# A two-layer encoder on one core: the opening laid out anew, the softmax's sums applied to the gates as rows, weight splits in pieces of 512 columns with half of the high parts on ScalarE, and a new order of issue

## The chip, the cores and the metric

The kernel runs on one core of a Trainium2 chip. The metric is the device time in microseconds (us) of one execution; lower is better. The core's engines are PE (TensorE), DVE (VectorE), ACT (ScalarE), POOL (GpSimd) and SP (SyncE, which here only issues DMAs). Each engine takes its instructions in the order in which they were issued and waits on semaphores of the others.

## The reference

All is float32; the sequence has 1024 tokens of width 1024, batch 1.

```python
c_act = jax.nn.silu(c)
for layer in range(DEPTH):                       # DEPTH = 2
    mod = c_act @ ada_w[layer] + ada_b[layer]
    shift, scale, gate = jnp.split(mod, 3, axis=-1)
    h = rms_norm(x, norm_w[layer]) * (1.0 + scale[:, None, :]) + shift[:, None, :]
    ...                                          # y = even_mixer(h) or odd_mixer(h)
    x = x + gate[:, None, :] * y
```

The result is the final RMSNorm of x. The even mixer (layer 0) projects h and runs two groups of attention side by side: A, eight query heads of 64 on two key and value heads, with rotary positions by row and column; and B, eight heads of latent attention, with compressed queries and a compressed key and value. Each is a dense softmax over all 1024 keys,

```python
p = jax.nn.softmax(sc, axis=-1)
oa = oa * jax.nn.silu(ga)
ob = mla_attention(q_lat, q_rope, ckv, k_rope, w_uv) * jax.nn.silu(gb)
return jnp.concatenate([oa, ob], axis=-1) @ w_out
```

and the outputs go through gates and one output projection. The odd mixer (layer 1) is attention in a window of 128 tokens to each side, with a penalty by distance and a learned sink per head, 16 heads on 4 key and value heads, then gate and output projection.

## The kernel before

**Products.** The data stay transposed, features on the 128 partitions. Every large product is made of three (`mm3`, L1112): a float32 operand is split into a high part (a cast to fp32r) and a low part (what is left), and high·high, high·low and low·high are added in PSUM. So each operand needs a cast and a subtraction on ACT, POOL or DVE before PE can use it. In the names an `h` or `l` at the end is the high or low part (`w30h`, `G7l`), and an `s` the weight as loaded (`wg7s`).

**Who decides the order.** All operations pass through `Recorder` (L586), which is why every row of the profile has one line, L1017 before: rows are told apart by the tiles. It records the operations, plans them with a cost for each (`cost`, L695), with pools of buffers (`u`: 52 tiles of 128x1024, `ua`: 3 of 128x512, `sm`: 32 of 128x16, eight PSUM banks) and with a rule (`held`, L932) by which a DVE operation with two inputs in SBUF and a POOL operation don't run at once. The order planned is then changed by hand: `placed` (L961) puts operation i right behind operation j for every pair of the table `PLACES` (L81), and `emit` (L1009) issues the result.

**Stages**, by the trace of before:
- 0 to 21 us, the opening. SP loads x by four chunks of two times 512 columns (`xT`), the small columns (`cols`), the first modulation weights (`ada`) and the first projection weights (`w30s`, `w10s`). PE runs transposes of the identity (`warm`, L1151), and turns SiLU(c) into the row `cb`. `xT_half` (L1358) squares x on ACT, adds halves on POOL and DVE (`sq`), and sums over partitions on PE, with a column `share` of 1/1024 as the moving operand (`mean_squares`, L1222): matmuls of 128x1. DVE adds epsilon (`ss`), POOL raises to the power −1/2 (`r`), PE transposes r into rows (`broadcast_rstd`, L1246), DVE multiplies x by them and ACT applies shift and scale (`modulate`, L1290, out: `hT00h`). The shift and scale of a chunk are sums of `ada` times `cb` on DVE, one 128x1024 operation each (`ada_sum`, L1186).
- 21 to 128 us: layer 0's projections; `wload` (L1318) loads and splits their weights.
- 128 to about 350 us: the gates' product by a scheme of seven products for eight. `g_load` (L1701) splits its weights (`wg0` to `wg15`, double tiles of 128x1024), `combine` (L1680) builds its sums of h (`hf`, `G4` to `G7`, `gk`) on DVE, `g_step` (L1741) issues the matmuls between those of attention. The gates stay in `gT`.
- 132 to 640 us: 16 groups A, then 16 groups B (`run_groups`, L1854), each one head and half the queries. `softmax_unit` (L1803) makes one tile of 128 queries by 1024 keys: PE's scores, DVE's maximum (`nm`), ACT's exponential with its sum (`Pa`, `Pb`, `sm`), DVE's reciprocal (`rs`), and POOL scales the tile by it. In the next group `pv_step` (L1832) transposes P by 128 keys, splits it (`hla`, `hlb`) and multiplies by V; for two of eight key tiles in groups B that is done ahead on POOL (`pv_ahead`, L1822). `pv_final` (L1844) adds two halves of the accumulator (`ot`, `og`) and POOL multiplies by the gate, 64 rows at a time.
- 640 to 705 us: layer 0's output (`wino_out`, L2271; `t30l`, `s30l`, `a220l` are its splits). To 760 us: layer 1's projections (`f_load`, L2498, splits `wf0` and on; `f_step`, L2523). To 1047 us: the windows (`win_S`, L2635, `win_PV`, L2668). To the end: layer 1's output (`xr`) and the last norm (`rbz`).

Weights that are sums of blocks pass through DRAM: POOL issues DMAs that add (`ws`, `gs`, `fs`), SP fetches the results.

Of the kernel before, what the change touches and what calls it, by code (L numbers as in the profile page):

```python
# [54 lines left out]
WARM = (18, 8, 6)  # L55
AHEAD = {"a": {}, "b": {4: 0, 7: 3}}
# [19 lines left out]
G_HI = "pool"  # L76
G_LO = "pool"
# [2749 lines left out]
```

## Time and profile before

| what | value |
|---|---|
| median of 3 runs | 1129.39 us (1127.12 to 1130.62) |
| the profiled execution | 1134.05 us, span 1132.2 us |
| mean granted clock of PE | 0.985 |
| busy: PE, DVE, ACT, POOL | 97%, 86%, 66%, 66% of the span |
| chain that ended last | PE 81%, DVE 12% |
| first product of the projections starts at | 20.75 us |
| POOL busy with scaling P (128 operations) | 154.7 us |
| POOL busy from 200 to 320 us | 107.51 of 120 us |

Busy time of PE counts from the issue of a matmul to its modelled end, so rows of neighbours overlap: what a matmul takes from PE is the distance of its start to the next one's. In a row of the timeline stand start, length, engine, line, operation, tiles written and read, shape, the number of instructions put together, and in brackets how long the engine idled before and what ended that. In a row of waits stand the total, the number of times and the longest.

### The profile page before, as it was taken

The numbers are of one execution on the slowest core, as the hardware profiler recorded it, in microseconds if no ns is written. First come the engines' busy times: TensorE is split into PE (matmuls) and PEld (weight loads), VectorE is DVE, ScalarE is ACT, GpSimd is POOL, SyncE is SP. The second block draws the span as 40 slices with busy tenths as digits, with TensorE's granted clock in tenths as the row PEclk, the third lists the DMA queues.
The fourth block names the chain that finished last, engine by engine and source line by source line (L and its number), as shares of the span: only waits on it lengthen the run. The fifth ranks groups of instructions, "written<-read, shape, count | busy, mean of one in ns | idle before, by whom it ended". The sixth has DMA issues, their size and how long they took to land.

```text
span 1132.2 us, 17617 instructions
## 1 busy us (share of the span) xinstructions
PE 1102.4 (97%) x5928; PEld 942.9 (83%) x5928; DVE 978.1 (86%) x1604; ACT 749.5 (66%) x1460; POOL 745.3 (66%) x732
## 2 busy tenths in 40 slices
PE   8999999999999999999999999999999999999996
PEld 7898877888887988888888877888888888888785
DVE  5978998898999988887888999998877787778995
ACT  4663554778777877887798742667776776766722
POOL 1135777988986737877879736757675775976422
PEclk7999999999999999999999999999999999999997
DMA  9869863564751486974785477401111221349303
GB/s 368 326 201 318 273 252 78 144 195 125 203 165 15 89 289 207 212 204 160 210 238 191 114 271 245 152 1 38 41 54 56 78 68 42 113 166 336 103 1 149
DMA packets 60026, 183.72 MB, mean 162 GB/s; under 512 B 7200, under 2 KB 9632, under 8 KB 58912
## 3 DMA queue, kind: packets, MB, share of 16 engines
q1 hardware_dynamic: 54464, 159.00, 40.2%
q0 software_dynamic: 4608, 22.02, 10.7%
q10 hardware_dynamic: 864, 1.57, 0.4%
q8 instruction: 47, 0.77, 0.3%
q14 instruction: 43, 0.35, 0.1%
HBM read 147.31 MB, written 70.91 MB: 193 GB/s over the span
## 4 chain that ended last, share of the span: by engine, by line
PE 81%; DVE 12%; issue 2%; ACT 2%; POOL 1%; DMA 1%; POOLq 0%; SPq 0%; DVEq 0%; ACTq 0%
PE psum L1017 81%; DVE nm L1017 1%; DVE xr L1017 1%; DVE hla L1017 1%; DVE t30l L1017 1%; DMA xT<-in_xt 1%; ACT Pb L1017 1%; DVE o L1017 0%; DVE T6l L1017 0%; DVE hlb L1017 0%; DVE s31l L1017 0%; DVE s30l L1017 0%; DVE psum L1017 0%; POOL sq L1017 0%; DVE t40l L1017 0%
## 5 line engine op out<-in xcount | busy, mean ns | idle before, releaser
L1017 DVE TENSOR_REDUCE nm<-psum 128x1 f32<-128x1024 f32 x128 | 155.6, 1219 | 21.0 <-PE psum L1017 18.8
L1017 POOL TENSOR_SCALAR Pa<-Pa,rs 128x1024 f32<-128x1024 f32 x64 | 77.4, 1233 | 34.9 <-DVE rs L1017 30.4
L1017 POOL TENSOR_SCALAR Pb<-Pb,rs 128x1024 f32<-128x1024 f32 x64 | 77.3, 1217 | 32.7 <-DVE rs L1017 29.7
L1017 POOL TENSOR_SCALAR p<-p,dn 128x384 f32<-128x384 f32 (+1 forms) x128 | 69.4, 560 | 33.2 <-DVE dn L1017 32.9
L1017 ACT ACTIVATE Pa<-psum,nm 128x1024 f32<-128x1024 f32 x64 | 71.6, 1119 | 27.6 <-DVE nm L1017 26.0
L1017 DVE TENSOR_TENSOR hla<-psum,hla 128x512 fp32r<-128x512 f32 x128 | 82.6, 683 | 4.4 <-ACT hla L1017 4.2
L1017 ACT ACTIVATE Pb<-psum,nm 128x1024 f32<-128x1024 f32 x64 | 71.9, 1124 | 20.2 <-DVE nm L1017 18.0
L1017 DVE CUSTOM_DVE_ANT_0 p<-psum,relt,sinkn 128x384 f32<-128x384 f32 (+1 forms) x128 | 70.4, 579 | 15.3 <-PE psum L1017 13.8
L1017 PE MATMUL psum<-hla,VA 128*128 128x512 f32 x256 | 80.5, 407 | 1.3 <-DVE og('0', 2)_631 L1017 1.1
L1017 ACT ACTIVATE p<-p,nm 128x385 f32<-128x385 f32 (+1 forms) x128 | 74.8, 591 | 10.2 <-DVE nm L1017 5.6
L1017 ACT CAST hla<-psum 128x512 fp32r<-128x512 f32 x128 | 70.5, 596 | 16.3 <-PE psum L1017 15.3
L1017 PE MATMUL psum<-k,q 128*128 128x512 f32 x256 | 80.5, 401 | 0.6 <-ACT Pb L1017 0.6
L1017 PE MATMUL psum<-hlb,VB 128*128 128x512 f32 x256 | 78.3, 409 | 0.5 <-DVE hlb L1017 0.5
L1017 PE MATMUL psum<-ident,Pa 128*128 128x128 f32 x512 | 73.4, 274 | 0.0
L1017 ACT CAST hl<-psum 128x512 fp32r<-128x512 f32 x88 | 48.7, 590 | 34.2 <-PE psum L1017 30.2
L1017 DVE TENSOR_TENSOR hlb<-psum,hlb 128x512 fp32r<-128x512 f32 x96 | 63.2, 684 | 8.7 <-ACT hlb L1017 8.2
L1017 PE MATMUL psum<-ident,Pb 128*128 128x128 f32 x512 | 70.3, 273 | 0.1
L1017 DVE TENSOR_TENSOR hl<-psum,hl 128x512 fp32r<-128x512 f32 x88 | 57.9, 686 | 12.9 <-ACT hl L1017 10.9
L1017 PEld LDWEIGHTS psum<-ident,Pa 128*128 128x128 f32 x512 | 61.4, 141 | 8.4 <-issue 0.2
L1017 PEld LDWEIGHTS psum<-ident,Pb 128*128 128x128 f32 x512 | 60.3, 140 | 9.0 <-ACT Pb L1017 0.5
L1017 ACT COPY ot<-psum 64x512 f32<-64x512 f32 x64 | 37.4, 584 | 39.6 <-PE psum L1017 38.5
L1017 ACT ACTIVATE sq<-xr 128x512 f32<-128x512 f32 (+2 forms) x30 | 19.3, 658 | 61.3 <-DVE xr L1017 61.3
(1152 smaller groups left out, 3845.3 us busy)
## 6 DMA issues: line engine op xcount, KB each, us to landing
ada<-in_ada_t SPq DMA_DIRECT2D x32, 512.0 KB, 8.1
fs<-in_w_f POOLq DMA_DIRECT2D x12, 768.0 KB, 9.2
adag<-in_ada_t SPq DMA_DIRECT2D x16, 512.0 KB, 5.3
ws<-in_w_out POOLq DMA_DIRECT2D x16, 512.0 KB, 6.5
S<-ws SPq DMA_DIRECT2D x16, 512.0 KB, 4.5
A<-in_w_out SPq DMA_DIRECT2D x12, 512.0 KB, 4.5
o<-spill SPq DMA_DIRECT2D x12, 512.0 KB, 5.5
fs<-in_w_f SPq DMA_DIRECT2D x6, 768.0 KB, 8.9
```

The costliest lines, as they stand in the source:

```text
L1017: fn(*[real(v) for v in a], **{k: real(v) for k, v in kw.items()})
```

## The change

**The opening.** ACT does all squares first. POOL adds the halves of chunk 0, DVE those of chunks 1 and 2 and then adds both halves of chunk 3 into chunk 2's sum; PE makes the sum over partitions with 12 calls instead of 20. Eight warming transposes stand before the first of them and 14 between the second and the third chunk's; the eight before r's transposes are gone. The shift of chunk 0 is no longer a DVE operation of 128x1024 but eight matmuls of 128x1 on PE, with an operand `ada_0` of the same size, laid out by the host, and a DVE operation of 128x1. A copy of r by DVE (`got`) stands before DVE's further sums and low parts. The first projection weights `w10` and `w30` come and are split in two halves each.

PE from the program's start, before and then after. `share,sq` are the sums over partitions, `cs,ada` the shift, `ident,r` r's transposes.

```order
L1017 MATMUL psum<-ident 128x128 x18
L1017 MATMUL psum<-ident,cs 128x128 x8
L1017 MATMUL psum<-share,sq_126 128x1 x4
L1017 MATMUL psum<-share,sq_127 128x1 x4
L1017 MATMUL psum<-share,sq_128 128x1 x4
L1017 MATMUL psum<-share,sq_129 128x1 x8
L1017 MATMUL psum<-ident 128x128 x8
L1017 MATMUL psum<-ident,r 128x128 x4
L1017 MATMUL psum<-ident 128x128 x6
L1017 MATMUL psum<-w30h_138,hT00h_91 128x512
```
```order
L1195 MATMUL psum<-ident 128x128 x18
L1195 MATMUL psum<-ident,cs 128x128 x8
L1195 MATMUL psum<-ident 128x128 x8
L1195 MATMUL psum<-share,sq_126 128x1 x4
L1195 MATMUL psum<-share,sq_127 128x1 x4
L1195 MATMUL psum<-ident 128x128 x14
L1195 MATMUL psum<-share,sq_128 128x1 x4
L1195 MATMUL psum<-cs,ada_131 128x1 x8
L1195 MATMUL psum<-ident,r 128x128 x4
L1195 MATMUL psum<-ident 128x128 x6
L1195 MATMUL psum<-w10h_136,hT00h_91 128x416
```

Eight sums over partitions have gone from behind the last square, and the eight matmuls of the shift stand between the mean and r's transposes.

**Layer 0's softmax.** P stays as the exponential. The four sums of a group stand in one tile; one reciprocal of 128x4 per group goes by a DMA on SP to DRAM, and once both heads of a pair have theirs, two DMAs on SP of 64x512 bring them back as rows over the partitions. POOL multiplies the gate by these rows (16 operations of 128x512) and then the heads' outputs by the gate, once per pair of heads (16 of 128x512 instead of 32 of 64x512). The rows take buffers of the pool `ua`, now four.

**Weight splits.** For the gates and for layer 1's features the parts are made in pieces of 512 columns; ACT casts the high parts of the first eight double tiles of each, POOL the others and all low parts.

POOL around the gates' weights `wg4` to `wg8`, before and after; `Pa<-Pa,rs` is the scaling of P.

```order
L1017 TENSOR_SCALAR wg4h<-wg4s 128x1024
L1017 TENSOR_SCALAR wg5h<-wg5s 128x1024
L1017 TENSOR_TENSOR wg4l<-wg4s,wg4h 128x1024
L1017 TENSOR_SCALAR Pa_355<-Pa_355,rs 128x1024
L1017 TENSOR_TENSOR wg5l<-wg5s,wg5h 128x1024
L1017 TENSOR_SCALAR wg6h<-wg6s 128x1024
L1017 TENSOR_TENSOR wg6l<-wg6s,wg6h 128x1024
L1017 DMA ws_317<-in_w_out 128x1024
L1017 TENSOR_SCALAR Pa_359<-Pa_359,rs 128x1024
L1017 TENSOR_SCALAR wg7h<-wg7s 128x1024
L1017 TENSOR_TENSOR wg7l<-wg7s,wg7h 128x1024
```
```order
L1195 TENSOR_TENSOR wg4l<-wg4s,wg4h 128x512 x2
L1195 TENSOR_TENSOR wg5l<-wg5s,wg5h 128x512 x2
L1195 TENSOR_TENSOR wg6l<-wg6s,wg6h 128x512 x2
L1195 TENSOR_TENSOR wg7l<-wg7s,wg7h 128x512 x2
L1195 TENSOR_SCALAR wg8h<-wg8s 128x512 x2
```

Scalings, casts and a DMA have gone from between the subtractions, which now follow each other.

**Order and constants.** `WINDOW` (how far ahead the planner looks) goes from 400 to 300, `SM_BUFS` from 32 to 12, `UA_BUFS` from 3 to 4, `RESERVE` of `sm` from 11 to 2; in `win_S` the maxima and the sums share a tile. `PLACES` has 638 lines instead of 460, and a new table `BANKS` gives PSUM banks by hand. The recorder is the same.

DVE at the end, before and after: `gcol` and `ngcol` are evictions of the last products, `rbz` the last norm's scaling of other columns.

```order
L1017 SCALAR_TENSOR_TENSOR xr_1908<-psum,gcol,xr_1908 128x2x256
L1017 SCALAR_TENSOR_TENSOR xr_1905<-psum,ngcol,xr_1905 128x256
L1017 SCALAR_TENSOR_TENSOR xr_1902<-xr_1902,cols,rbz_1979 128x512 x2
L1017 SCALAR_TENSOR_TENSOR xr_1901<-xr_1901,cols,rbz_1979 128x512
L1017 SCALAR_TENSOR_TENSOR xr_1904<-xr_1904,cols,rbz_1979 128x512
L1017 SCALAR_TENSOR_TENSOR xr_1905<-psum,ngcol,xr_1905 128x256 x2
L1017 SCALAR_TENSOR_TENSOR xr_1906<-psum,ngcol,xr_1906 128x256
```
```order
L1195 SCALAR_TENSOR_TENSOR xr_1709<-psum,gcol,xr_1709 128x2x256
L1195 SCALAR_TENSOR_TENSOR xr_1704<-xr_1704,cols,rbz_1780 128x512
L1195 SCALAR_TENSOR_TENSOR xr_1705<-xr_1705,cols,rbz_1780 128x512
L1195 SCALAR_TENSOR_TENSOR xr_1706<-psum,ngcol,xr_1706 128x256
L1195 SCALAR_TENSOR_TENSOR xr_1709<-psum,gcol,xr_1709 128x2x256
L1195 SCALAR_TENSOR_TENSOR xr_1702<-xr_1702,cols,rbz_1780 128x512
L1195 SCALAR_TENSOR_TENSOR xr_1705<-xr_1705,cols,rbz_1780 128x512
L1195 SCALAR_TENSOR_TENSOR xr_1706<-psum,ngcol,xr_1706 128x256
L1195 SCALAR_TENSOR_TENSOR xr_1707<-psum,ngcol,xr_1707 128x256
```

Of four scalings between the first eviction and the next, two stand ahead of the first now, and an eviction (`gcol`) stands between.

The diff, cut to its core:

```diff
-UA_BUFS = 3
-SM_BUFS = 32
+UA_BUFS = 4
+SM_BUFS = 12
...
-WARM = (18, 8, 6)
-AHEAD = {"a": {}, "b": {4: 0, 7: 3}}
+WARM = (18, 8, 14, 6)
+AHEAD = {"a": {}, "b": {4: 0, 7: 3}, "1": {}}
...
-G_HI = "pool"
-G_LO = "pool"
+G_ACT = 8
+F_ACT = 8
...
 PLACES = (
-    (95, 39), (92, 95), (127, 45), (167, 127), (164, 167), (234, 161), (231, 234), (96, 57), (237, 229), (304, 237),
...
@@ ada_mods
+            if turn and j:
+                s = U("ada0")
+                load(s, ada_0)
+                ps = PA("ada0")
+                for i in range(8):
+                    m_ = mm(ps[:, 0:1], lhsT=s[:, i * P:(i + 1) * P], rhs=cs[:, 8 + i:9 + i], start=i == 0, stop=i == 7)
+                    m_.deps.update(o.i for o in turn)
+                    turn = [m_]
+                marks["turn"] = turn
+                nc.vector.scalar_tensor_tensor(out=mods[:, 2 * k + j:2 * k + j + 1], in0=ps[:, 0:1], scalar=scale, in1=first,
+                                               op0=ALU.mult, op1=ALU.add)
+                continue
...
@@ broadcast_rstd
-        around = warm(WARM[1], around) if around else []
+        if around:
+            got_ = SM("got")
+            marks["got"] = nc.vector.tensor_copy(got_[:, 0:nt], r[:, 0:nt])
+        around = around or []
...
@@ wload
+            if late:
+                for o in (0, n // 2):
+                    c = slice(o, o + n // 2)
+                    load(s[:, c], w[:, c])
+                    nc.scalar.copy(h[:, c], s[:, c])
+                    sub(l[:, c], s[:, c], f(h[:, c]))
+                    rec.ops[-1].deps.add(late.i)
+                    res.append((h[:, c], l[:, c]))
+                continue
...
@@ xT_half
+            for k2 in range(3):
+                nc.scalar.activation(sq[k2], xT[0][k2], AF.Square)
+            for e in range(2):
+                nc.scalar.activation(part(3, e), xT[0][3][:, e * 512:(e + 1) * 512], AF.Square)
+            plus(nc.gpsimd, part(0, 0), part(0, 1))
+            plus(nc.vector, part(1, 0), part(1, 1)).deps.update(o.i for o in copied)
+            plus(nc.vector, part(2, 0), part(2, 1))
...
+            for e in range(2):
+                plus(nc.vector, part(2, 0), part(3, e))
+            m_ = add(part(2, 0), True)
...
+    def parts_of(s, h, l, n, eng):
+
+        for o in range(0, n, 512):
+            c = slice(o, o + 512)
+            if eng is nc.scalar:
+                nc.scalar.copy(h[:, c], s[:, c])
+            else:
+                hi_pool(h[:, c], s[:, c])
+            nc.gpsimd.tensor_tensor(out=l[:, c], in0=s[:, c], in1=f(h[:, c]), op=ALU.subtract)
...
+        parts_of(s, h, l, 1024, nc.scalar if d < G_ACT else nc.gpsimd)
...
@@ softmax_unit
-            nc.scalar.activation(pt, S, AF.Exp, bias=nm[:, 0:1], accum_out=sm[:, 0:1])
+            nc.scalar.activation(pt, S, AF.Exp, bias=nm[:, 0:1], accum_out=sums)
+        return pt
...
-        nc.vector.reciprocal(r[:, 0:1], sm[:, 0:1])
-        nc.gpsimd.tensor_scalar(pt, pt, r[:, 0:1], 1.0, op0=ALU.mult, op1=ALU.mult)
-        return pt
...
+    def keep_sums(p, e, half, sums):
+
+        r = SM("rs")
+        nc.vector.reciprocal(r[:, 0:4], sums)
+        nc.sync.dma_start(out=rs_sp[p][e:e + 1, half * 512:(half + 1) * 512].rearrange("o (q j) -> (o q) j", j=4),
+                          in_=r[:, 0:4])
+        if e:
+            c = slice(half * 512, half * 512 + 512)
+            rows[p, half] = UA(f"rows{p}{half}")
+            for e in range(2):
+                load(rows[p, half][e * 64:e * 64 + 64, :], rs_sp[p][e:e + 1, c].partition_broadcast(64)[:, 0])
+
+    def scale_gate(p, half, gate):
+
+        c = slice(half * 512, half * 512 + 512)
+        by_tile = gate[:, c].rearrange("p (j q) -> p j q", j=4)
+        nc.gpsimd.tensor_tensor(out=by_tile, in0=by_tile, in1=rows.pop((p, half)).rearrange("p (q j) -> p j q", j=4), op=ALU.mult)
...
@@ pv_final
-        nc.gpsimd.tensor_tensor(out=og[r, c], in0=og[r, c], in1=gate[r, c], op=ALU.mult)
+        if h % 2:
+            nc.gpsimd.tensor_tensor(out=og[:, c], in0=og[:, c], in1=gate[:, c], op=ALU.mult)
...
@@ run_groups
+                keep_sums(g["p"], g["h"] % 2, g["half"], sums[:, 0:4])
             if prev is not None:
+                if prev["h"] % 2:
+                    scale_gate(prev["p"], prev["half"], prev["gate"]())
...
@@ f_load
-        hi_pool(h[:, 0:w], s[:, 0:w])
-        nc.gpsimd.tensor_tensor(out=l[:, 0:w], in0=s[:, 0:w], in1=f(h[:, 0:w]), op=ALU.subtract)
+        parts_of(s, h, l, w, nc.scalar if d < F_ACT else nc.gpsimd)
```

More of the change, by code (lines that the diff above doesn't have):

```diff
@@ L1166, in encoder_kernel @@
     cb = U("cb")
-    copied = []
+    copied, turned = [], []
     for j in range(2):
@@ L1315, in modulate, with wload @@
                 nc.scalar.activation(keep, src, AF.Identity, bias=sh_col(l, kc))
-    def wload(ws, ncol, name, hi_eng="pool", mark=None, lo_eng="dve"):
+    def wload(ws, ncol, name, hi_eng="pool", mark=None, lo_eng="dve", late=None):
         res = []
@@ L1363, in xT_half @@
             pt, add = mean_squares("x0", 4)
-            for k2 in range(4):
-                q = U(f"sq0{k2}")
-                a, b = q[:, 0:512], q[:, 512:1024]
-                if k2 < 3:
-                    nc.scalar.activation(q, xT[0][k2], AF.Square)
-                    (nc.vector if k2 == 1 else nc.gpsimd).tensor_tensor(out=a, in0=a, in1=b, op=ALU.add)
-                    if k2 == 1:
-                        rec.ops[-1].deps.update(o.i for o in copied)
-                else:
-                    nc.scalar.activation(a, xT[0][k2][:, 0:512], AF.Square)
-                    nc.scalar.activation(b, xT[0][k2][:, 512:1024], AF.Square)
-                for t in (a,) if k2 < 3 else (a, b):
-                    m_ = add(t, k2 == 3 and t is b)
+            sq = [U(f"sq0{k2}") for k2 in range(4)]
+            part = lambda k2, e: sq[k2][:, e * 512:(e + 1) * 512]
+            plus = lambda eng, a, b: eng.tensor_tensor(out=a, in0=a, in1=b, op=ALU.add)
+            for k2 in range(3):
[5 more added lines that the diff above has]
+            plus(nc.vector, part(2, 0), part(2, 1))
+            w_ = warm(WARM[1], turned)
+            for k2 in range(2):
+                m_ = add(part(k2, 0))
+                for o in rec.ops[m_.i - 3:m_.i + 1]:
+                    o.deps.update(x.i for x in w_)
+                w_ = [m_]
+            w_ = warm(WARM[2], w_)
+            for e in range(2):
+                plus(nc.vector, part(2, 0), part(3, e))
+            m_ = add(part(2, 0), True)
             for o in rec.ops[m_.i - 3:m_.i + 1]:
-                o.dur = 427
-            ada_mods(0, 0)
-            return rstd_of_means(pt, 4, "x0", around=[m_], sums=rec.ops[-1])
+                o.deps.update(x.i for x in w_)
+            ada_mods(0, 0, turn=[m_])
+            return rstd_of_means(pt, 4, "x0", around=marks["turn"], sums=marks["sum"])
         else:
@@ L1489, in encoder_kernel @@
             ada_mods(0, kc, late=marks["rstd", "x0"])
+            for o in rec.ops[-3:]:
+                if o.eng == "DVE":
+                    o.deps.add(marks["got"].i)
         c = chunk(xT[0], kc)
@@ L1798, in encoder_kernel, with softmax_unit @@
     gTT.update(combine(H_(0, 0), H_(0, 1), H_(1, 0), H_(1, 1), "G", G_ENG))
-    def softmax_unit(qk, name):
+    def softmax_unit(qk, name, sums):
         S = PS(f"S{name}")
@@ L1813, in softmax_unit, with ahead @@
         pt = U(f"P{name}")
[L1814 removed]
         with rec.at(shift=PRIO["exp"]):
[L1816 to L1826 removed]
+            nc.scalar.activation(pt, S, AF.Exp, bias=nm[:, 0:1], accum_out=sums)
+        return pt
+    rs_sp = [dr.tile([2, 1024], F32, name=f"rs_sp{p}") for p in range(8)]
+    rows = {}
+    def keep_sums(p, e, half, sums):
+        r = SM("rs")
+        nc.vector.reciprocal(r[:, 0:4], sums)
[10 more added lines that the diff above has]
+        nc.gpsimd.tensor_tensor(out=by_tile, in0=by_tile, in1=rows.pop((p, half)).rearrange("p (q j) -> p j q", j=4), op=ALU.mult)
+    def ahead(parts, last_, name):
+        pt = PT(f"T{name}")
+        transposes(lambda j: pt[:, j * P:(j + 1) * P], parts, last_)
+        hl = UR(f"hl{name}")
+        t = UA(f"t{name}")
         nc.scalar.copy(t, pt)
@@ L1947, in encoder_kernel @@
             groupsA.append(dict(
-                name=f"a{h}{half}", h=h, half=half, qk=qk_of,
+                name=f"a{h}{half}", h=h, half=half, p=h // 2, qk=qk_of,
                 V=lambda kt, g=g: VA[kt // 4][:, kt % 4, g, :, :].rearrange("p s d -> p (s d)"),
@@ L2114, in encoder_kernel @@
             groupsB.append(dict(
-                name=f"b{h}{half}", h=h, half=half, qk=qk_of,
+                name=f"b{h}{half}", h=h, half=half, p=4 + h // 2, qk=qk_of,
                 V=lambda kt, h=h: VB[h // 4, kt // 2][:, kt % 2, h % 4, :, :].rearrange("p s d -> p (s d)"),
@@ L2669, in win_PV @@
         acc = PV(f"pv1_{g}{i}")
+        early = {}
         for t in range(n):
             kt = lo + t
-            pt = PT(f"T1_{g}{i}{t}")
-            transposes(lambda j: pt[:, j * P:(j + 1) * P],
-                       [Ps[j // 2][:, (j % 2) * 512 + t * P:(j % 2) * 512 + t * P + P] for j in range(4)], T1_LAST)
-            hl = UR(f"hl1_{g}{i}{t}")
-            with rec.at(shift=PRIO["hi1"]):
-                nc.scalar.copy(hl[:, 0:512], pt)
-            with rec.at(shift=PRIO["lo1"]):
-                sub(hl[:, 512:1024], pt, f(hl[:, 0:512]))
+            parts = lambda t_: [Ps[j // 2][:, (j % 2) * 512 + t_ * P:(j % 2) * 512 + t_ * P + P] for j in range(4)]
+            for t2 in AHEAD["1"]:
+                if AHEAD["1"][t2] == t:
+                    early[t2] = ahead(parts(t2), T1_LAST, f"1_{g}{i}{t2}")
+            hl = early.get(t)
+            if hl is None:
+                pt = PT(f"T1_{g}{i}{t}")
+                transposes(lambda j: pt[:, j * P:(j + 1) * P], parts(t), T1_LAST)
+                hl = UR(f"hl1_{g}{i}{t}")
+                with rec.at(shift=PRIO["hi1"]):
+                    nc.scalar.copy(hl[:, 0:512], pt)
+                with rec.at(shift=PRIO["lo1"]):
+                    sub(hl[:, 512:1024], pt, f(hl[:, 0:512]))
             V = V1[kt // 2][:, kt % 2, g].rearrange("p s d -> p (s d)")
```

72 lines of the change are left out of this document (32 added, 40 removed), and 1051 rows, old and new, of the table PLACES.

## The prediction

> **What bounds the kernel now.** First the page: its span and busy times, PE's clock over forty slices, and the shares of the chain that ended last.
>
> ```profile
> span 1132.2 us, 17617 instructions
> PE 1102.4 (97%) x5928; PEld 942.9 (83%) x5928; DVE 978.1 (86%) x1604; ACT 749.5 (66%) x1460; POOL 745.3 (66%) x732
> PEclk7999999999999999999999999999999999999997
> PE 81%; DVE 12%; issue 2%; ACT 2%; POOL 1%; DMA 1%; POOLq 0%; SPq 0%; DVEq 0%; ACTq 0%
> ```
>
> PE is busy 97% of the span, and the change keeps its products (it takes out 8 calls for sums and adds 14 warming transposes and 8 narrow matmuls). So no edit can win more than PE's pauses and the stretches in which its clock is low. Both are few. Two views name them: what PE waited for from 350 to 1110 us (us in total, times, longest; the first and the last of seven rows, 7.8 us in all), and windows (length, PE busy, granted clock) around the stretches of low clock, outside which it is 1.00.
>
> ```profile
> PE psum L1017 <- DVE xr L1017: 2.8, 2, 1.7
> ...
> PE psum L1017 <- DVE hlb L1017: 0.5, 1, 0.5
> ```
> ```profile
> 8.40:22.00 13.60, 12.02 (x53) 0.50 1.03 412
> 179.05:182.45 3.40, 3.40 (x10) 0.50 0.00 0
> 342.90:346.30 3.40, 3.00 (x9) 0.50 0.00 0
> 1114.30:1121.10 6.80, 6.11 (x28) 0.50 0.79 311
> ```
>
> Most of these pauses are PE waiting for DVE; the longer ones, at 176, 340 and 1112 us, are shown below, and each of the three low stretches after the opening follows one of them. So the kernel is bound by PE, and what is left to win is where DVE hands a bank or an operand over late. The profiled execution took 1134.05 us, 1.85 outside its span and 4.66 above the median of 1129.39. I sum against 1134.05 and take 4.66 off at the end. About 0.3% (3.4 us) is what a measurement of this kernel can tell from no change, so faster means below 1126.0, slower above 1132.8.
>
> **The opening.** The timeline's rows (start, length):
>
> ```profile
> 7.19 0.69 DVE L1017 TENSOR_TENSOR sq<-sq 128x512 f32<-128x512 f32 x1
> 9.71 1.15 ACT L1017 ACTIVATE sq<-xT 128x512 f32<-128x512 f32 x2 [0.18 <-DMA xT<-in_xt]
> 10.93 5.28 PE L1017 MATMUL psum<-share,sq 128*128 128x1 f32 x24 [1.10 <-POOL sq L1017]
> 11.13 1.35 DVE L1017 CUSTOM_DVE_ANT_0 ada<-ada,cb,a 128x1024 f32<-128x1024 f32 x1 [3.25 <-DMA ada<-in_ada_t]
> 16.48 1.96 POOL L1017 TENSOR_TENSOR r<-ss,mhalf 128x4 f32<-128x4 f32 x1 [5.61 <-DVE ss L1017]
> 18.49 1.11 PE L1017 MATMUL psum<-ident,r 128*128 128x128 f32 x4 [0.48 <-POOL r L1017]
> 20.75 0.79 PE L1017 MATMUL psum<-w30h,hT00h 128*128 128x512 f32 x1
> ```
>
> The squares end at 10.86, and the first real product starts at 20.75. Between lie 24 one-column matmuls of 0.22 us (12 calls, each recorded twice), r on POOL and its transposes, which end 1.15 before the product. After the change, squares and their DMAs come as before; two DVE adds of 0.69 follow (12.24), then 4 calls, 8 records: 1.76 us at 0.22, to 14.0. DVE's remaining sum of 1.35 ends at 13.6, so it doesn't delay the mean. Adding epsilon and r: r took 1.96 beside DVE's w30l, and the change makes that work wait for r; I take 1.3 and have r at 15.6. PE meanwhile does the shift's 8 calls: 16 records at 0.22 are 3.5 us, to 17.5. They become the late thing: transposes to 18.6, product at 19.75, **1.0 earlier**. If the 14 transposes lift the clock, the narrow matmuls take half: the mean ends at 13.1, r at 15.2, which then ends last, transposes at 15.7, product at 16.9: **3.9 earlier**. The clock probably falls again meanwhile, since one-column matmuls filled much of 8.4 to 22.0 at 0.50; products at half rate until 22.0 give back up to half of what was won. I take −2, ends −0.5 and −4. The new copy of r on DVE waits for POOL; queued behind it are the first weights' low parts, x's scaling and all later sums of DVE, and PE waits for none of them before r's transposes are done. The shift's new operand comes by a load as large as the one it replaces, in its place on SP. The halves of the first weights cost two more issues there and nothing on PE's path as long as x's scaling is the later operand; otherwise half a low part, some 0.7 (half of the 1.35 that a DVE operation on 1024 columns took above), is to be added, and it lies within the smaller end.
>
> The Trainium skill, "TensorE: Matmul & The Clock Gate", Part 1, says that about 3.4 us of sustained work lift the clock and an idle window of that length lowers it; by that, 14 transposes might open full rate and the opening would give the larger end. The row of 13.60 us at 0.50 speaks against counting narrow matmuls as work.
>
> **Layer 0, 128 to 200 us.** DVE, POOL and PE around the longest pause before the end:
>
> ```profile
> 171.06 2.87 DVE L1017 TENSOR_TENSOR G7l<-hf,G7h 128x1024 fp32r<-128x1024 f32 x1
> 173.85 3.39 DVE L1017 TENSOR_TENSOR G4l<-hf,G4h 128x1024 fp32r<-128x1024 f32 x1
> 181.15 1.23 DVE L1017 TENSOR_TENSOR G5l<-hf,G5h 128x1024 fp32r<-128x1024 f32 x1
> ```
> ```profile
> 171.53 1.32 POOL L1017 TENSOR_SCALAR wg7h<-wg7s 128x1024 fp32r<-128x1024 f32 x1
> 172.93 3.23 POOL L1017 TENSOR_TENSOR wg7l<-wg7s,wg7h 128x1024 fp32r<-128x1024 f32 x1
> ```
> ```profile
> 178.63 0.50 PE L1017 MATMUL psum<-G7h,wg6h 128*128 128x512 f32 x1 [2.77 <-DVE gk L1017]
> ```
>
> G7l and G4l take 2.87 and 3.39 beside POOL's weight splits; the same operation with POOL idle took 1.23. The bank's sums stand behind them, PE pauses 2.77, and then comes a window of 3.40 us at 0.50, half of it lost, 1.7: 4.5 together. The change takes every scaling of P and the first eight high casts from POOL. Without blocking the two DVE operations last 2.5 instead of 6.1, more than the pause. But G7l, G4l and the sums keep their order, and POOL now has eight low pieces of 512 columns in a row. I take −4, ends 0 and −4.5.
>
> The Trainium skill, "SBUF — State Buffer", SBUF: two separate sides, says that DVE and GpSimd exchange their shared port pair by whole instructions. By that, shorter pieces alone would bound a wait at one piece. The next rows don't show this: three POOL operations ran within one DVE operation.
>
> **320 to 350 us.**
>
> ```profile
> 336.44 3.64 DVE L1017 TENSOR_TENSOR krt<-krt 128x256 f32<-128x256 f32 x1
> ```
> ```profile
> 336.73 1.06 POOL L1017 TENSOR_SCALAR wuqh<-wuqs 128x768 fp32r<-128x768 f32 x1
> 337.53 1.26 POOL L1017 TENSOR_SCALAR ckvTh<-lat 128x1024 fp32r<-128x1024 f32 x1
> 338.55 1.25 POOL L1017 TENSOR_SCALAR cqTh<-lat 128x1024 fp32r<-128x1024 f32 x1
> ```
> ```profile
> 340.94 0.47 PE L1017 MATMUL psum<-hla,VA 128*128 128x512 f32 x1 [1.14 <-DVE og('0', 2)_631 L1017]
> 343.30 0.79 PE L1017 MATMUL psum<-khh,Qa 128*128 128x512 f32 x1 [1.20 <-DVE hla L1017]
> ```
>
> A small addition is held 3.64 us while POOL casts; two pauses (1.14, 1.20) and 3.40 us at half clock follow: 4.0. In the new order krt still stands between two reductions, and POOL still has a run of casts. Half goes: −2, ends 0 and −4.
>
> **350 to 1110 us.** The seven waits of the list sum to 7.8. Splits by ScalarE in layer 1 and a freer POOL bear on the features' low parts and the waits in groups; the layer-0 output keeps its POOL work. A third goes: −2.5, ends 0 and −6.
>
> **The end.**
>
> ```profile
> 1110.40 0.48 DVE L1017 SCALAR_TENSOR_TENSOR xr<-psum,ngcol,xr 128x256 f32<-128x256 f32 x1 [3.53 <-PE psum L1017]
> 1110.81 3.74 DVE L1017 SCALAR_TENSOR_TENSOR xr<-xr,cols,rbz 128x512 f32<-128x512 f32 x4
> 1114.47 1.26 DVE L1017 SCALAR_TENSOR_TENSOR xr<-psum,ngcol,xr 128x256 f32<-128x256 f32 x3
> ```
> ```profile
> 1114.99 0.58 PE L1017 MATMUL psum<-b221l,s41h 128*128 128x256 f32 x1 [2.83 <-DVE xr L1017]
> ```
>
> DVE idles 3.53, then does four long operations between two evictions, and PE pauses 2.83. In the new order two of the four stand ahead of the first eviction, in that idle time; between remain two and one eviction more, 1.87 and about 0.7, so the next eviction comes 1.1 sooner. Whether the 6.80 us at half clock (3.4 lost) go too is open: −2, ends −1 and −4.5.
>
> **New work and waits.**
>
> ```profile
> L1017 POOL TENSOR_SCALAR Pa<-Pa,rs 128x1024 f32<-128x1024 f32 x64 | 77.4, 1233 | 34.9 <-DVE rs L1017 30.4
> L1017 ACT CAST hla<-psum 128x512 fp32r<-128x512 f32 x128 | 70.5, 596 | 16.3 <-PE psum L1017 15.3
> spill<-og SPq DMA_DIRECT2D x6, 512.0 KB, 3.0
> q<-qr_sp SPq DMA_DIRECT2D x16, 128.0 KB, 4.5
> ```
> ```profile
> L1017 POOL TENSOR_TENSOR hlb<-tb,hlb 128x512 fp32r<-128x512 f32 x32 | 41.7, 1306 | 1.7
> L1017 POOL TENSOR_SCALAR hlb<-tb 128x512 fp32r<-128x512 f32 x32 | 23.9, 748 | 14.8 <-ACT tb L1017 12.3 <-PE psum L1017 1.9 <-POOL og('0', 4)_904 L1017 0.4
> ```
>
> ScalarE takes on 16 casts of 512 columns in each layer, at 0.6 some 10 us each time; at 66% busy, and with its products' casts served in order, that costs nothing as long as it is spread over the 70 us in which the weights come; where a cast stands ahead of an exponential, 0.6 is added. POOL loses 154 us of scalings (twice the 77.4 of Pa, Pb being as many) and gains 16 multiplications of 1.3, of which nothing was on PE's path. The row of sums goes out and comes back by SP: an estimate of 3.0 + 4.5 = 7.5 us by these two transfers, against some 16 us of a group (32 groups from 128 to 640). But on SP the loads of rows wait for that landing and for a free ScalarE buffer, with weights, q and k queued behind; on POOL the multiplication waits for the rows, with hlb's halves for PE behind it. I take +1, ends 0 and +16.
>
> **Sum.** −2 −4 −2 −2.5 −2 +1 = −11.5: 1122.5 for a profiled execution, less 4.66 is **1118**.
>
> **The rivals.** (a) *The pauses only move*: runs of POOL work hold DVE as they held krt, the clock falls as before. The opening's −1 to −2, −2 elsewhere and +2 of new waits leave 1127 to 1131, within 0.3%. For it: same order of G7l, G4l, krt. Chance 0.14. (b) *Rows come late*, slower: from where a row lands more than a group's 16 us after its sums, POOL stands and hlb's 0.75 + 1.31 comes late to PE. In 8 groups B that is 16.5, plus half of it in groups A by weights late on SP: 1133 to 1142. Against it are the 8 us to spare. Chance 0.10. (c) *All the named pauses go*: −4 −4.5 −4 −7.8 −4.5 is −24.8, 1105. For it: nearly all blocked DVE operations lie beside work that POOL loses. Chance 0.14. My forecast, 1108 to 1126: 0.62.
>
> **How the numbers follow.** Faster is the forecast and (c), 0.76; same 0.14; slower 0.10. The range of 1104 to 1132 leaves out (b) and the far ends.
>
> **What would show it.** Right: first product between 17 and 20 us; no pause of PE over 2 us and clock 1.00 near 180 us; G7l near 1.3 us; krt short or two pauses left; POOL's busy time near 600 us. Wrong: PE waiting for POOL's hlb or for a DMA between 150 and 640 us, new stretches of 0.50, or SP's waits at rows as long as a group.

## The result and the profile after

The changed kernel takes 1115.47 us (median of 9 runs, 1114.29 to 1124.74), the kernel before 1130.32 in the 9 runs beside it: a ratio of 0.9889, 95% interval 0.9859 to 0.992. It is faster: the medians differ by 14.9 us, and the interval allows 9 to 16; 1118 was forecast. The profiled execution of the changed kernel took 1120.33, 13.7 less than that of before and 4.9 above its own median. The page's first lines:

```profile
span 1118.6 us, 17496 instructions
PE 1095.1 (98%) x5942; PEld 939.7 (84%) x5942; DVE 937.3 (84%) x1513; ACT 767.4 (69%) x1494; POOL 585.9 (52%) x661
PEclk8999999999999999999999999999999999999998
```

POOL's busy time has fallen by 159 us and PE's by 7. PE's idle time (the span less its busy time) has fallen from 29.8 to 23.5, and the windows at half clock behind the opening, without the one in which both spans end, from 13.6 to 3.4 us, in which half of the time is lost: some 5 us less. Together these are some 11 of the 13.6 us by which the span is shorter. A page of shares alone would not show where that time was won. For that I take the same matmul in both traces and compare its start, or the end of the span. The lead is how much earlier it comes than before:

| landmark of PE | before | after | lead | lead of a second execution, without the pause at 136 us |
|---|---|---|---|---|
| first product of the projections | 20.75 | 17.97 | 2.8 | 4.8 |
| first w2h product (layer 0's projections) | 61.94 | 60.31 | 1.6 | 3.6 |
| last G7l x wg6h (gates) | 182.61 | 178.84 | 3.8 | 10.8 |
| last G5l x wg13h (gates) | 358.02 | 352.54 | 5.5 | 12.1 |
| last wuqh x cqTh (rotary queries) | 378.25 | 373.51 | 4.7 | 11.3 |
| first hT10h x wf0h (layer 1's features) | 715.79 | 708.72 | 7.1 | 12.1 |
| last kh x Q (windows) | 1017.72 | 1011.12 | 6.6 | 11.6 |
| end of the span | 1132.19 | 1118.55 | 13.6 | 18.6 |

The last column is the profile of the run after_again below, whose span is 1113.6. From 182 to 358 us the two gain about the same (1.7 and 1.3), and the end is worth 7.0 in both. From 378 to 716 us they differ, 2.4 against 0.8. PE makes the same pause for ScalarE's exponential in both; behind it the clock stays full in the profiled execution and falls to a half in the second. The rows and the windows behind them (length, then busy time of PE, its weight loads, DVE, ACT and POOL with the number of instructions, then granted clock, busy share of the DMA engines, GB/s):

```profile
400.06 0.50 PE L1195 MATMUL psum<-khh,Qa 128*128 128x512 f32 x1 [2.05 <-ACT Pa L1195]
400.00:403.40 3.40, 3.33 (x15) 2.74 (x16) 2.79 (x3) 3.36 (x7) 0.00 (x0) 1.00 0.88 127
```
```profile
393.45 0.53 PE L1195 MATMUL psum<-khh,Qa 128*128 128x512 f32 x1 [2.00 <-ACT Pa L1195]
393.80:397.20 3.40, 3.40 (x10) 2.66 (x9) 1.57 (x2) 2.92 (x6) 0.00 (x0) 0.50 0.88 119
```

So a pause of this length costs 1.7 us more in some executions than in others, and a lead of one execution is uncertain by that much. What PE waited for in the whole span, after:

```profile
PE psum L1195 <- ACT Pa L1195: 4.0, 3, 2.0
PE psum L1195 <- POOL wg1l L1195: 3.3, 1, 3.3
PE psum L1195 <- DVE xr L1195: 2.3, 2, 1.7
PE psum L1195 <- DVE og('0', 2)_584 L1195: 1.4, 1, 1.4
```

The wait for gk (2.8) and the long one for xr are gone; a wait for POOL's wg1l is new, and PE now waits 4.0 us for ScalarE's exponentials, where before it waited 1.2. The windows of granted clock:

```profile
6.40:13.10 6.70, 6.05 (x54) 5.73 (x53) 5.30 (x9) 3.30 (x5) 0.80 (x1) 1.00 1.01 389
13.20:19.90 6.70, 6.70 (x28) 6.06 (x28) 3.78 (x9) 3.79 (x7) 0.94 (x1) 0.50 1.03 415
139.50:142.80 3.30, 3.30 (x8) 2.62 (x9) 0.00 (x0) 0.00 (x0) 1.10 (x1) 0.50 1.03 417
```

In the opening the clock is full to 13.1 and half to 19.9; of the three later low stretches that the prediction shows none is left, and one has come at 139 us, behind the new pause. The opening, the gates and the pause at 136 us in the timeline after:

```profile
11.74 1.05 PE L1195 MATMUL psum<-share,sq 128*128 128x1 f32 x8 [0.65 <-DVE sq L1195]
12.65 3.14 PE L1195 MATMUL psum<-cs,ada 128*128 128x1 f32 x16
13.10 1.04 POOL L1195 TENSOR_TENSOR r<-ss,mhalf 128x4 f32<-128x4 f32 x1 [5.90 <-DVE ss L1195]
15.66 1.09 PE L1195 MATMUL psum<-ident,r 128*128 128x128 f32 x4
17.97 0.71 PE L1195 MATMUL psum<-w10h,hT00h 128*128 128x416 f32 x1
...
133.64 1.30 POOL L1195 TENSOR_TENSOR wg3l<-wg3s,wg3h 128x512 fp32r<-128x512 f32 x1 [5.24 <-ACT wg1h L1195]
139.42 0.79 PE L1195 MATMUL psum<-hT00h,wg1l 128*128 128x512 f32 x1 [3.34 <-POOL wg1l L1195]
...
168.48 1.22 DVE L1195 TENSOR_TENSOR G7l<-hf,G7h 128x1024 fp32r<-128x1024 f32 x1
172.81 1.22 DVE L1195 TENSOR_TENSOR G4l<-hf,G4h 128x1024 fp32r<-128x1024 f32 x1
...
333.54 0.41 DVE L1195 TENSOR_TENSOR krt<-krt 128x256 f32<-128x256 f32 x1
```

G7l and G4l take 1.22 where they took 2.87 and 3.39, krt 0.41 where it took 3.64. r is ready at 14.14, but its transposes stand behind the sixteen narrow records and start at 15.66. POOL stood 5.24 us ahead of wg3l; the releaser that the row names, ScalarE's cast of wg1, cannot be it: wg3l does not read it, and it had ended at 132.86. The instruction waits for DMAs too, and the store q_sp<-qz, issued at 119.00, took 14.5 to land: 133.5. That this store is what POOL waited for is argued from the times here; the run wg1_first below has a row that names it.

### The profile page after: what moved, and what is told of

It is laid out like the page before. It is cut to its first block, busy times and chain, and to the rows that moved or that the text cites. A ratio compares the mean times of both kernels' runs of the same rounds, so it can differ in the third digit from the quotient of the medians.

```text
span 1118.6 us, 17496 instructions
## 1 busy us (share of the span) xinstructions
PE 1095.1 (98%) x5942; PEld 939.7 (84%) x5942; DVE 937.3 (84%) x1513; ACT 767.4 (69%) x1494; POOL 585.9 (52%) x661
## 4 chain that ended last, share of the span: by engine, by line
PE 83%; DVE 9%; POOL 2%; issue 2%; DMA 2%; ACT 1%; SPq 0%; POOLq 0%; ACTq 0%; DVEq 0%
PE psum L1195 83%; DVE ada L1195 1%; DVE hla L1195 1%; DVE xr L1195 1%; DVE nm L1195 1%; DMA xT<-in_xt 1%; DMA S<-ws 1%; DMA qr_sp<-qrh 1%; DVE hT00l L1195 1%; ACT Pa L1195 1%; DVE hT11l L1195 0%; POOL r L1195 0%; DVE psum L1195 0%; DVE s10l L1195 0%; DVE xT L1195 0%
## 5 line engine op out<-in xcount | busy, mean ns | idle before, releaser
L1195 ACT ACTIVATE Pa<-psum,nm 128x1024 f32<-128x1024 f32 x64 | 71.5, 1119 | 20.2 <-DVE nm L1195 19.7
L1195 ACT ACTIVATE Pb<-psum,nm 128x1024 f32<-128x1024 f32 x64 | 71.9, 1123 | 16.3 <-DVE nm L1195 15.2
L1195 ACT ACTIVATE p<-p,dn 128x385 f32<-128x385 f32 (+1 forms) x128 | 74.9, 591 | 9.5 <-DVE dn L1195 5.4
L1195 POOL TENSOR_SCALAR hlb<-tb 128x512 fp32r<-128x512 f32 x32 | 22.6, 708 | 91.8 <-ACT tb L1195 91.6
L1195 PE MATMUL psum<-ident,Pa 128*128 128x128 f32 x512 | 70.4, 273 | 0.2 <-DVE hla L1195 0.2
L1195 DVE TENSOR_TENSOR hl<-psum,hl 128x512 fp32r<-128x512 f32 x88 | 58.1, 686 | 14.5 <-ACT hl L1195 13.1
L1195 PE MATMUL psum<-hl,V 128*128 128x512 f32 x176 | 58.3, 397 | 0.0
L1195 ACT CAST hlb<-psum 128x512 fp32r<-128x512 f32 x96 | 53.4, 599 | 1.9 <-PE psum L1195 1.5
```

Of the source, the lines that this page charges most:

```text
L1195: fn(*[real(v) for v in a], **{k: real(v) for k, v in kw.items()})
```

## The experiments

All are compared with the changed kernel, 1115.47 (9 runs) and 1116.36 when run again; the ratios are to the kernel before. Where not said otherwise, the order that the changed kernel issues is kept word for word and only what is named differs.

**no_warm14.** The 14 transposes between the sums are not issued.

```diff
             w_ = warm(WARM[2], w_)
+            rec.skip.update(range(len(rec.ops) - WARM[2], len(rec.ops)))
```

> The changed kernel with its order of issue kept, without the 14 warming transposes between the second and the third chunk's sums (they compute nothing that is used). If they lift the clock for the last sums, as the prediction's larger end has it: the 8 records of the third sum at 0.22 instead of 0.13 us each, r and the first product 0.5 to 1.0 us later than 17.97, and 0.5 to 1.5 us in all. The rival, that the clock there does not hang on them: first product at 17.97 within 0.2, the time the same.

Measured: 1115.06, ratio 0.9862 (0.9832 to 0.9891). The opening behaves as the first theory says, the total as the rival:

```profile
11.30 1.87 PE L1205 MATMUL psum<-share,sq 128*128 128x1 f32 x8 [1.57 <-DVE sq L1205]
13.03 3.55 PE L1205 MATMUL psum<-cs,ada 128*128 128x1 f32 x16
18.75 0.71 PE L1205 MATMUL psum<-w10h,hT00h 128*128 128x416 f32 x1
```

The last sums take 1.87 instead of 1.05 at half clock and the first product comes 0.8 later than 17.97. But the same opening with the transposes gave 15.93 to 21.70 in other executions (below), so one profile does not show that the transposes did it, and the time does not either.

**shift_dve.** Chunk 0's shift as a DVE sum behind ss, no narrow matmuls; the diff in short.

```diff
-                    m_ = mm(ps[:, 0:1], lhsT=s[:, i * P:(i + 1) * P], ...)      # eight times, and a DVE operation of 128x1
+                nc.vector.tensor_tensor_reduce(out=s, in0=s, in1=cb, ..., accum_out=mods[...])   # right behind ss
```

> The changed kernel with the shift of chunk 0 back on DVE as one sum of 128x1024 right behind ss, and PE's eight narrow matmuls (16 records, 12.65 to 15.66 in the profile after) left out. If those matmuls are the late thing in the opening, as the prediction has it: r's transposes start at about 14.3 instead of 15.66, the first product at 16.6 to 17.0 instead of 17.97, 0.5 to 1.4 us less in all. The rival: DVE's sum of 1.3 beside POOL's r stretches r from 1.04 towards the 1.96 of before and holds the copy of r, the transposes start no more than 0.5 earlier, and the time is the same.

Measured: 1116.01, 0.9878 (0.985 to 0.9907): the rival. DVE and POOL, then PE:

```profile
13.16 1.28 DVE L1205 CUSTOM_DVE_ANT_0 ada<-ada,cb,cols 128x1024 f32<-128x1024 f32 x1
13.33 2.01 POOL L1205 TENSOR_TENSOR r<-ss,mhalf 128x4 f32<-128x4 f32 x1 [6.17 <-DVE ss L1205]
15.39 1.11 PE L1205 MATMUL psum<-ident,r 128*128 128x128 f32 x4 [2.38 <-POOL r L1205]
```

r takes 2.01 beside DVE's sum and 1.04 alone; it ends 0.90 after the sum. The transposes start 0.27 earlier than with the narrow matmuls, the first product 0.32 earlier (17.65). So these are the last wait where they stand, but in their place r comes late, and taking them away is worth a quarter of a microsecond.

**hi_pool.** The high casts of the split weights on POOL again.

```diff
-                nc.scalar.copy(h[:, c], s[:, c])
+                nc.gpsimd.tensor_scalar(h[:, c], s[:, c], 1.0, 0.0, op0=ALU.mult, op1=ALU.add)
```

> The changed kernel with the 32 pieces of high casts (16 in layer 0, about as many in layer 1) put back from ScalarE to POOL, at the same places in the order. Theory that POOL's work beside DVE's operations with two inputs makes PE's pauses: G and hf operations of DVE get longer between 150 and 200 us, 1 to 4 us more there; but the pause of 3.3 us at 136 us, where POOL waits for ScalarE's cast of wg1, gets shorter, so -3 to +3 in all. Rival, that the casts' engine is off PE's path altogether: the same pauses, the same time within 1 us.

Measured: 1120.67, 0.9908 (0.9878 to 0.9939), 4 to 5 us more than the changed kernel and outside both expectations. The intervals overlap, so the traces have to tell more. Up to 182 us the lead is 8.5, with no pause at 136; from 645 to 1018 us it falls from 8.8 to 4.2, where the changed kernel run again keeps 10.0 and then 11.6. POOL, DVE and PE there:

```profile
686.90 3.36 POOL L1205 TENSOR_TENSOR s40l<-S,s40h 128x1024 fp32r<-128x1024 f32 x1
687.95 2.87 DVE L1205 TENSOR_TENSOR sq<-sq,sq 128x512 f32<-128x512 f32 x1
692.77 0.63 PE L1205 MATMUL psum<-ident,sq 128*128 128x128 f32 x4 [1.54 <-DVE sq L1205]
```

The addition sq takes 0.68 in the changed kernel (at 691.71). Five casts of `wf` ahead of s40l on POOL push it beside DVE's sq, and PE waits for that. The same happens again 26 us later, and costs more:

```profile
715.05 2.86 DVE L1205 TENSOR_TENSOR wv1l<-wv1s,wv1h 128x1024 fp32r<-128x1024 f32 x1
718.66 0.30 PE L1205 MATMUL psum<-ident,sq 128*128 128x128 f32 x1 [2.42 <-DVE sq L1205]
```

Here wv1l, 1.21 in the changed kernel, holds the next sq, and from 720.0 on PE runs 3.4 us at half clock. The two pauses and half of that window are 5.7 us. So ScalarE's casts pay in layer 1, where the theory holds. In layer 0, where it was placed, DVE's operations get longer too (a G6l takes 2.32 for 1.22), but PE does not wait for them: from the first wg0h product to the last G7l product the lead grows by 7.4 us, as much as in after_again.

**scale_back.** POOL scales P again, by ones, behind each exponential.

```diff
+        rec.extra[e_.i] = [(nc.gpsimd.real.tensor_scalar, (pt, pt, one[:, 0:1], 1.0), dict(op0=ALU.mult, op1=ALU.mult))]
```

> The changed kernel with POOL scaling each P tile again, now by 1.0: 128 operations of 128x1024 directly behind the exponentials, all else in the same order; the result does not change. Theory of the prediction (POOL's load blocks DVE, DVE is late for PE): POOL busy about 155 us more, DVE's operations with two SBUF inputs stretched again, pauses of PE and low clock between 130 and 400 us come back, 4 to 12 us more. Rival (PE is the bound and the new order made the gain, POOL's load is beside the path): 0 to 2 us more.

Measured: 1193.98, 1.0562 (1.053 to 1.0594), 78 us more, far over both. PE's waits:

```profile
PE psum L1205 <- POOL Pa L1205: 11.7, 8, 4.7
PE psum L1205 <- POOL Pb L1205: 8.7, 7, 2.2
PE psum L1205 <- POOL hlb L1205: 8.0, 5, 3.0
```

From 128 to 640 us 40 us of PE's waits name POOL and 8 name DVE, and the mean granted clock there falls from 1.00 to 0.95. PE waits for POOL itself more than for a DVE that POOL blocks: in an order without a place for them the scalings hold what stands behind them on POOL. So the run does not test the theory, and its size says nothing about a planned scaling; plan_scaled does.

**wg1_first.** Four operations moved by number: wg1's casts and low parts earlier.

```diff
+        self.move += [([1091, 1093], 1324), ([1092, 1094], 1069)]     # what, behind which
```

> The changed kernel with four operations moved: ScalarE's two casts of wg1's high parts stand two Qa evictions earlier, and on POOL wg1's low parts stand ahead of wg3's and of r, right behind the small operation on sscq. In the profile after, POOL stood 5.24 us before wg3l until 133.64, about when the store q_sp<-qz (issued 119.0, landed after 14.5) had left the buffer, and PE then paused 3.3 us for wg1l at 136 us and ran 3.4 us at half clock. If that store's late landing is what some executions pay (median 1115, but three of nine at 1120 and one at 1125): no pause at 136 us in any execution, all runs at 1114 to 1116, the median 0 to 1 us lower than 1115.5. Rival, that the pause comes from ScalarE's casts or POOL's order: 3 to 5 us less in every execution, a median near 1111. Second rival, that the slower executions have another cause: still a third of the runs at 1120.

Measured: 1116.17, 0.986 (0.9837 to 0.9884); six runs between 1115.64 and 1116.79. That is what the first theory expects: no low clock at 140 us and no run near 1120, though the median is not lower and PE pauses 0.98 for another tile (cqraw) at 139 us. But six runs are few, and the run tuned below has the same four moves and three of its six runs at 1120.5 to 1121.5: a slower execution can have another cause too. Now the row names the store:

```profile
131.51 3.53 POOL L1206 TENSOR_TENSOR wg1l<-wg1s,wg1h 128x512 fp32r<-128x512 f32 x2 [2.88 <-DMA q_sp<-qz]
```

It was issued at 119.40 and landed after 11.9. In the profiles where it took 14.5 (after) and 14.9 (end_old) PE paused over 3 us at 136 to 139; where it took 8.5 to 10.3 (no_warm14, shift_dve, hi_pool) it did not. Before the change it took 14.5 as well (issued at 122.86), in an order in which PE made no such pause. Why it lands late in some executions was not found.

**end_old.** Two scalings of the last norm put back behind the first eviction.

```diff
+        self.move += [([9371, 9374], 9375)]
```

> The changed kernel with two of the last norm's scalings on DVE (xr<-xr,cols,rbz, 128x512, 0.7 us each in the profile after) put back behind the first ngcol eviction, so that four stand between it and the next one as before the change. If the order of DVE at the end is worth what the profile shows (pause 0.64 after against 2.83 before): the second eviction 0.7 to 1.4 us later, a pause of 1.5 to 2.2 us, 0.7 to 1.4 us more in all, and up to 4 us more if the pause lowers the clock again. Rival, that the end's gain (about 7 us from the last projection's start on) comes from somewhere else, such as shorter DVE operations beside an idle POOL: the same time within 0.5 us.

Measured: 1120.13 (1115.85 to 1130.46), 0.9904 (0.9871 to 0.9937). The end's lead is 4.0 instead of 7.0:

```profile
1106.40 3.77 DVE L1206 SCALAR_TENSOR_TENSOR xr<-xr,cols,rbz 128x512 f32<-128x512 f32 x4
1110.10 1.26 DVE L1206 SCALAR_TENSOR_TENSOR xr<-psum,ngcol,xr 128x256 f32<-128x256 f32 x3
```
```profile
1111.41 0.39 PE L1206 MATMUL psum<-b221h,s41h 128*128 128x256 f32 x1 [2.16 <-DVE xr L1206]
```
```profile
1112.20:1115.50 3.30, 3.30 (x18) 3.30 (x17) 0.97 (x3) 0.73 (x2) 0.00 (x0) 0.50 0.23 89
```

The pause is 2.16 for 0.64, and a window at half clock follows it: 1.5 and 1.7 us, about the 3.0 that the end loses. This is the theory, in the upper half of its range. The total says less: the median is 4.7 above the changed kernel's, but the eight runs spread over 15 us, the intervals overlap, and the profiled execution is the slowest of them (1130.46), late in the opening and at 143 us as well.

**after_plan, before_plan, plan_scaled.** The planner's own order: the tables of places and banks empty (before_plan takes the planner's banks as they are); plan_scaled with the scaling of P as a recorded operation.

```diff
 PLACES = (
-    ...
 )
```

> The changed kernel in the planner's own order: both tables, of places and of banks, empty; the operations are the same. If the gain is in the operations (less work on POOL), this keeps more than half of it against the kernel before: 1115 to 1123. If it is in the order made by hand: 1130 to 1150, as slow as before or slower.

> As the run in the planner's own order, with POOL scaling each P tile by 1.0 as an operation that the planner knows and places (128 of 128x1024, some 155 us of POOL). If POOL's load is what makes DVE and so PE late: 5 to 15 us above the run in the planner's own order without it, though not the 78 us that the scaling cost where no place had been planned for it. Rival, that POOL has room for it once the order allows for it: within 2 us of that run.

> The kernel before in the planner's own order: its table of places empty, banks as the planner gave them. After the change the planner's own order took 1187, 71 more than the one made by hand. If the operations of the change are what helps (POOL with 31% less work), this takes 1195 to 1215, near the 1206 that the planner's order took with P scaled. If the operations are worth nothing and only the hand-made orders differ: 1185 to 1190.

Measured: after_plan 1186.89 (ratio 1.0481, 1.0452 to 1.051), before_plan 1185.66 (1.0482, 1.0453 to 1.0511), plan_scaled 1205.85 (1.065, 1.0622 to 1.0678). The kernel before has a table of places (437 lines, against 615 after) and one of banks too, so neither table is new. The busy times of the first two, where POOL has 601.6 and 751.6 us:

```profile
PE 1127.3 (95%) x5942; PEld 939.1 (79%) x5942; DVE 949.7 (80%) x1513; ACT 765.6 (65%) x1494; POOL 601.6 (51%) x661
```
```profile
PE 1122.4 (95%) x5928; PEld 937.9 (79%) x5928; DVE 974.4 (82%) x1604; ACT 750.1 (63%) x1460; POOL 751.6 (63%) x732
```

after_plan is far above both of its expectations, plan_scaled somewhat above its first one (19 us for 5 to 15), and before_plan lies where its second one has it, which calls the operations worth nothing. With 150 us less on POOL the planner's order is no faster. The orders made by hand take 71 us off the operations of after and some 54 off those of before. Yet the scaling alone costs 19 us in a planned order. If such costs add, the operations of the change win about 19 by the scaling and lose as much by the rest (the rows' way through SP, pieces, constants). That is argued, not shown: the rest was not taken apart, each run is one order of a planner that makes another order for other operations, and the two don't choose banks by the same rule. No run gives the operations of before a new order made by hand, so how the 15 us divide between operations and order stays open.

**rows_twice.** Each load of a row of sums is issued twice.

```diff
+                rec.extra[l_.i] = [l_.call]
```

> The changed kernel with each load of the rows of sums issued twice (32 more DMAs of 64x512 on SP in its queue, same data). If the rows are on the path, as the rival of a slower result had it: POOL's multiplications and what is queued behind on SP come 1 us or more later per pair, 5 to 16 us more. The prediction's theory, that they have some 8 us to spare: the same time within 1 us.

Measured: 1146.9, 1.0147 (1.0116 to 1.0178), 31 us more, twice the rival's upper end. The second load writes the same tile, so SP waits for the first to land, a wait that the changed kernel does not have. SP's waits from 128 to 640 us, then ScalarE and PE at one place:

```profile
SPq L1205 <- DMA rows<-rs_sp: 132.3, 29, 8.0
```
```profile
464.55 1.08 ACT L1205 CAST hlb<-psum 128x512 fp32r<-128x512 f32 x2 [5.75 <-DMA k<-knp]
465.19 1.22 PE L1205 MATMUL psum<-hlb,VB 128*128 128x512 f32 x2 [4.58 <-ACT hlb L1205]
```

Late are not the rows but the loads k<-knp queued behind them on SP, and by them a buffer that ScalarE's cast of hlb needs. PE makes four pauses of this size, 4.58 to 5.33, each with 6.8 us at half clock: 33 us, about the whole loss, though only this one was followed back to SP. So the run shows what it costs to hold SP, not that the rows of the changed kernel come late. That kernel has the same queue, but SP stands for the rows' stores only 9.7 us in all (longest 7.1), and though POOL waits 28 us for rows, no wait of PE between 150 and 640 us names POOL.

**after_again, tuned.** The changed kernel once more, and five moves in its order.

```diff
+        self.move += [([1091, 1093], 1324), ([1092, 1094], 1069), ([3047, 3050], 3014), ([5875], 5728), ([6310, 6198], 6568)]
```

> The changed kernel again, unchanged, beside the three others of this call. Both theories of its spread (a late store at 136 us, a late start of the projections) expect the same here: a median of 1114 to 1121, most runs near 1115, some at 1120. If runs at 1120 are an affair of one chip: all at 1115.

> The changed kernel with five moves in its order: wg1's casts and low parts earlier as in the run of that name; on DVE wuql behind og and the next maximum (a pause of 1.4 us at 348 us in the profile after), t10l behind the first eviction xr after it (1.7 at 679), and two evictions of V ahead of T7l (1.0 at 748). If these pauses are DVE operations held by POOL standing ahead of what PE waits for, and nothing else comes late in their place: 2 to 4 us less than the changed kernel, 1111 to 1114, and no runs at 1120. Rival, that another wait takes their place at once: within 1 us of 1116.

Measured: 1116.36 (1114.48 to 1119.12; 0.9874, 0.985 to 0.9897) and 1118.95 (1115.59 to 1121.47; 0.9891, 0.9866 to 0.9916). Two of the six runs of after_again are at 1119, so they are not all near 1115, as they would be if the spread were one chip's. The moves bring nothing that the runs can tell, and three runs of tuned are at 1120.5 to 1121.5, where none was expected. The pauses at 348 and 679 us end, but others stand in their place: 2.27 for ScalarE's Pa at 346 us (only one of two maxima was moved ahead of wuql), with a window of half clock behind it, and 1.42 for V at 741 us. PE's first row of waits tells it:

```profile
PE psum L1206 <- ACT Pa L1206: 6.3, 4, 2.3
```

## Why the prediction was right, point by point

- **What bounds it.** Right: PE is at 98%, and some 11 of 13.6 us came from pauses and low clock. The sum, 11.5, stands against 13.7 between the profiled executions, but it comes so near in part by luck: the end gave nearly 4 us more than forecast, and the new waits took 4 us more.
- **The opening**, −2 forecast: the lead at the first w2h product is 1.6. In nine other profiles with this opening or nearly this it lies between −1.7 (end_old, which changes only the end) and 3.6, and only one execution of the kernel before was profiled, so the size is not settled. The narrow matmuls are the last wait, as the prediction had it, with r at 14.14 instead of 15.2 or 15.6. (The 15.2 adds 2.1 to the mean's end where the other case adds 1.6; with 1.6 it is 14.7, and the narrow matmuls come last there too.) By the run shift_dve taking them away wins 0.27, as r then takes 2.01 beside DVE. What the 14 transposes do stays open.
- **128 to 200 us**, −4 forecast: mis-sized, and two things in one. The blocking is gone as argued (1.22 for 2.87 and 3.39; the row of 1.23 that the prediction reads as POOL idle had a scaling of P start 0.16 us into it, but 1.22 is also what the operation takes elsewhere). It is worth more: from the first wg0h product to the last G7l product the lead grows from 3.4 to 10.8 in after_again, 7.4 us, the pauses of before at 137 (0.69) and 157 to 159 us (1.26) among them. In the profiled execution the new wait for wg1l and its half clock give back 5.2. My rival's run of eight low pieces never came about: POOL waits for ScalarE between them.
- **320 to 350 us**, −2: 1.7 and 1.3 from one landmark to the next (182 to 358 us). krt was short, and one pause of 1.4 behind wuql took the place of two.
- **350 to 1110 us**, −2.5: about right in the profiled execution (5.5 to 6.6 up to 1018 us, and the pause of 1.10 at 1069 is gone), but by luck. In after_again the lead falls from 12.1 to 11.6 over the same stretch, with the half clock at 394 us. It is a difference of two: from 358 to 378 the lead falls by 0.8, with new waits for Pa of 4.0 in all up to 400 us, which the prediction did not have; from 378 to 716 it rises by 2.4. hi_pool shows that without ScalarE's casts layer 1 would lose some 6 us, by one profile of each.
- **The end**, −2: too small, the term that was most wrong in size. With the 1.1 of the pause at 1069 counted above, it is 5.9: 2.2 less pause and 3.4 of half clock. The prediction left open whether the clock's fall would go, and took 1.1 of pause and a quarter of the clock. end_old brings back 3.0 of it by two operations, so about half of this gain is shown to hang on their place; the rest is read from the traces.
- **New waits**, +1: 5.2 in the profiled execution and none of that kind in after_again, but not by the way priced. It is a store holding a buffer, not the rows. The prediction's own sign of being wrong, a new stretch of 0.50, did come there. The rows' estimate of 7.5 us was short: their stores and loads have medians of 3.5 and 5.9 to landing, 9.4 together.
- **The rivals.** (b), rows late on SP, did not come. rows_twice shows what a held SP would do, with k's loads as the victims, where the prediction spoke of hlb behind POOL. So what mattered was not the 8 us that a row had to spare but how long SP is held. (c) has 12.5 up to 358 us, the forecast 8: six of eight profiles of the changed order, edited runs among them, have 8.9 to 13.2 there, the profiled execution 5.5 and end_old −0.1. What the prediction did not ask is whether the operations or the order win: with the planner's order the changed operations win nothing.

## What to carry to other kernels

In a kernel bound by PE, look for the few operations that another engine's run of work stretches just where PE waits, and price a pause with the low clock behind it: here the clock was more than half of what the end was worth. An operation taken off an engine need not win anything until the order is made anew for it, as here in the planner's order; measure both in the planner's order and in the tuned one. Profile more than one execution before explaining a microsecond or two. Before adding small DMAs to a queue, name what is queued behind them and which buffers those free.

## What the runs showed of the hardware

The first low stretch of the clock differed between executions of nearly the same opening: from 13.1 to 19.9 us in the profiled execution, and in after_again and in end_old as in the two rows below. The first product comes at 17.97, 15.93 and 21.70.

```profile
15.00:18.30 3.30, 3.05 (x10) 2.33 (x9) 3.30 (x8) 2.82 (x5) 0.00 (x0) 0.50 1.03 407
```
```profile
9.70:23.30 13.60, 13.60 (x60) 13.07 (x61) 6.96 (x15) 5.57 (x10) 1.04 (x1) 0.50 1.03 408
```

These stretches last two, one and four times 3.4 us. The Trainium skill, "TensorE: Matmul & The Clock Gate", Part 1, says that the activity window of about 3.4 us runs freely, so that the start of a kernel meets it at any phase; these profiles agree. The Trainium skill, "TensorE: Matmul & The Clock Gate", HAM oscillation, gives the rule that PE should have no idle gap of more than about 3.4 us. Here pauses of 2.77, 2.83, 2.16 and 3.34 us were each followed by half clock, so in this kernel shorter ones can cost it. They need not: pauses of 2.05 (after, at 400 us), 2.16 (hi_pool, at 396 us) and 2.94 us (before_plan, at 464 us) were followed by full clock. What decides between the two was not found.
